# Two-layer hybrid decoder on one core: ACT's weight roundings placed behind evacuations, the pooling mixer pipelined over three advances per pair of up products, the order at attention's start and end changed

## The chip, the core and the metric

One core of one Trainium2 chip runs the whole program. The engines named below are PE (matrix products), DVE (vector), ACT (scalar, activations), POOL (GpSimd) and SP, which issues the DMAs. The metric is the device time of one execution in microseconds (us), taken as the median over executions; a smaller number is better.

## The reference, cut to what matters

Two layers over 1040 tokens (16 meta tokens and 1024 others) of width 1024. Layer 0 mixes with latent attention (16 heads), layer 1 with a pooling mixer of four groups of 256 channels. Behind each mixer stands a gated MLP with a causal convolution of width 3 over the tokens. Every part has an RMS norm before and after it.

```python
for i in range(2):
    a = rmsnorm(h, norm_mix_pre[i])
    m = mla_mixer(a, ...) if i == 0 else pool_mixer(a, w_group, scale)
    h = h + rmsnorm(m, norm_mix_post[i])
    f = conv_ffn(rmsnorm(h, norm_ffn_pre[i]), ...)
    h = h + rmsnorm(f, norm_ffn_post[i])

# pool_mixer, per group g with window w = 2, 4, 8, 16:
means = (csum - csum shifted by w) / min(t, w)
y[g] = (means[g] - h[g]) @ w_group[g]              # 256 x 256
# conv_ffn
u = h @ w_up                                        # 1024 x 5632
u = conv_b + sum(conv_w[j] * up[:, j:j + L] for j in range(3))
gate, val = split(u); return (silu(gate) * val) @ w_down
```

## The kernel before

**Number format.** Every matrix product is made of three: both operands are split into a rounded high part and the rest. For a weight tile, ACT makes the high part (`wh<-wr`, L64), DVE the low part (`wl<-wr,wh`, L70), and PE then runs wh·xh, wh·xl and wl·xh into PSUM (L764).

**Stages, in order.** Down projections of attention (`ps_d`, 5 to 85 us); attention (85 to 545 us), of which `open_attention` returns the opening steps (projections of the first heads) and `attention` runs 48 blocks, three query blocks of up to 348 tokens for each of 16 heads; the output projection `wo(0)` and `wo(1)` (545 to 643 us) for two halves of the tokens (536 and 504); then for each layer and each half: `ffn_up` part 0, `ffn_down` part 0, `ffn_up` part 1, `ffn_down` part 1. A part of `ffn_up` is 11 pairs of products (gate and value), so 22 *up products*. In layer 0, half 1, an up product is 24 matmuls over 506 columns; in layer 1, half 0 it is 48 matmuls over 260 or 262 columns. An up product's PSUM result is taken out by ACT (`cv`, L908: the first tap and the bias) and twice by DVE (`cv<-ps_m`, L912: the other taps); these three are called the evacuation here.

**Attention.** A block's scores (`ps_s`, L534 to L536; `score_tile`), softmax (DVE L543 and L551, ACT L548, POOL L553), transposes (`ps_t`, L585) and value products (`ps_o`, L570 and L571; `value_steps`) are queued so that the scores of the next block stand between the value steps of the present one (`merge`). The scores of block (0, 0) are emitted at the start of `attention`, after the opening steps. The last head's blocks run as 0, 1, 2, so that the last block has nine value steps and no scores beside them. A finished head goes to memory (`heads<-o`, L577) and comes back as operand of `wo` (`or<-heads`, L703). `wo(0)` starts its first three output tiles without the last 128 rows of the operand (`early`).

**Background work.** Norms, residual additions and the pooling mixer are generators (`after_mixer`, `after_ffn`, `post`, `pre`, `poolmix`). `tick()` advances the first of them to its next `yield`, with the priority of an instruction 200 places earlier in the program. Ticks stand between products: two per pair of up products, one per output tile of `ffn_down`, two per tile of `wo`; `drain()` runs the rest between the stages. `poolmix` shapes a group's two 128-channel slices on DVE (`pa` L1027, running sums `psm` L1037, `pmx` L1040, small corrections L1043 and L1044), splits them (`xh` on ACT, `xl` on DVE), and then emits the group's matmuls. It runs twice, each time inside part 0 of the `ffn_up` of that time: for half 0 during layer 0, half 1 (24 matmuls over 268 columns per group; the stretch from 1039 to 1199 us, called pool 1 here), and for half 1 during layer 1, half 0 (12 matmuls over 504 columns per group; 1441 to 1591 us, pool 2).

**What sets the order.** A scheduler walks the program once, with those priorities, and fixes for each engine one queue. At run time an engine takes its queue in order and waits where an operand is late. `issue_after(x)` queues what it holds behind instruction x. In the kernel before, a weight tile's rounding is queued as soon as the scheduler finds room, up to five up products ahead.

**PSUM.** Six banks serve the products: `banks(2)` makes three tiles of two banks, for half 0, `banks(1)` six tiles of one, for half 1.

Of the kernel before, what the change touches and what calls it, by code (L numbers as in the profile page):

```python
# [11 lines left out]
F32 = mybir.dt.float32  # L12
# [8 lines left out]
T = NMETA + SEQ  # L21
# [25 lines left out]
class Kern:  # L47
# [270 lines left out]
    def open_attention(self, es):  # L318
# [12 lines left out]
        return [rs[0], ks[0], rs[1], qs[0], ks[1], *vs[:4], qs[1], rs[2], ks[2], qs[2], *vs[4:]]  # L331
# [8 lines left out]
    def attention(self, es):  # L340
        tc, nc, io = self.tc, self.nc, self.io
        if True:
# [173 lines left out]
    def score_tile(self, h, b, i):  # L516

        nc, ap, sm = self.nc, self.ap, self.aq
# [4 lines left out]
        P = self.aq.tile([QT, min(T, 348 * (b + 1))], F32, tag=f"P{b}", name="P", bufs=3)  # L523
# [35 lines left out]
    def value_steps(self, h, b, P):  # L559
# [19 lines left out]
        def step(j):  # L579
# [13 lines left out]
            if j % self.PM == 1 and not (h == NH - 1 and b == 2):  # L593
# [13 lines left out]
    def dense(self):  # L607
# [3 lines left out]
        self.fp, self.up, self.tp = P("fp", 8), P("up", 2), P("tp", 5)  # L611
# [4 lines left out]
        self.dtile = lambda x: self.tp.tile([128, HALF], F32R, tag="x" + x, name="diag", bufs=2)  # L616
        self.H, self.A, self.bg = {}, {}, []
# [40 lines left out]
    def after_mixer(self, hf, F, acc, L, pre):  # L658
        acc = yield from self.post(hf, F, acc, G_MIXPOST + 8 * L)
        if pre:  # L660

            self.late = yield from self.inv_rms_steps(acc, "xh", 2)
            yield from self.pre(hf, L, True)
        else:
            yield from self.ffn_norm(hf, acc)
# [44 lines left out]
    def wtile(self, src, nk, pool=False):  # L710
        nc = self.nc
        n = 128 * nk
# [11 lines left out]
        self.split(r[:, :n], hi[:, :n], lo[:, :n], lo_eng="dve")  # L724
# [43 lines left out]
    def evac(self, dst, ps, scale=None):  # L768
        c0 = 0
        for p in ps:  # L770
            d = dst[:, c0:c0 + p.shape[1]]
            if scale is None:
                self.nc.scalar.copy(d, p)  # L773
            else:
                self.nc.scalar.activation(d, p, AF.Copy, scale=scale)
            c0 += p.shape[1]

    def addsq(self, acc, t):

# [11 lines left out]
    def wo(self, hf):  # L791
# [14 lines left out]
        for m in range(KD):  # L806
# [3 lines left out]
            else:  # L810
                ps = self.mm_half(self.wtile(io["w_o"][m], KD), *O)
# [3 lines left out]
            self.evac(f, ps)  # L815
# [71 lines left out]
    def ffn_up(self, hf, part):  # L887
# [8 lines left out]
        for jj in range(JH):  # L896
            j = part * JH + jj
            cv = []
            for gv in range(2):
                idx = gv * NJ + j  # L900
                u, = self.mm_half(self.wtile(io["w_up"][L, j, :, gv], KD), ah, al, skip=skip)
                if (L, hf) == (0, 0):
                    t = self.up.tile([128, HALF], F32, tag="u", name="u")
# [4 lines left out]
                nc.scalar.activation(c, u[:, pad:pad + n], AF.Identity, bias=self.par(p0 + 3), scale=self.par(p0 + 2))  # L908
# [18 lines left out]
    def ffn_down(self, part, G, F):  # L927
# [3 lines left out]
        src = lambda m, k0, nk: self.wtile(io["w_down"][L, part, m, :, k0:k0 + nk], nk)  # L931
# [181 lines left out]
```

## Time and profile before

| | us |
|---|---|
| median of 3 runs | 2242.7 (2241.12 to 2243.98) |
| the profiled execution's own time | 2243.88 |
| its span in the trace | 2242.1 |
| PE busy | 2153.3 (96% of the span) |
| DVE busy | 1466.7 (65%) |
| ACT busy | 1045.3 (47%) |
| POOL busy | 382.7 (17%) |

The busy time of an engine is the union of its instructions, so a PE that runs at half its clock is as busy as one at full clock. The granted clock (PEclk) stands beside it: 1.00 is 2.4 GHz, 0.50 is 1.2 GHz, a value between them is a stretch that had both. Over the whole span it is 0.982. Where the queue of PE stands still, the bracket at a row names the instruction that came last before it went on.

### The profile page before, as it was taken

To read this page: it belongs to the slowest core of one execution; us is meant where nothing else is said; L and a number is where in the kernel's file an instruction comes from. 1 tells how busy PE (TensorE), PEld (TensorE's weight loads), DVE (VectorE), ACT (ScalarE), POOL (GpSimd) and SP (SyncE) were. 2 spreads that over 40 slices of the span, in tenths; PEclk is the share of its full clock that TensorE was granted. 3 is DMA by queue.
4 is the path that set the end of the run, shared out by engine and by line. 5 is a ranking of instruction groups with operands and counts; after the bars stand their busy time and mean duration, and the time that the engine had idled before them with its cause. 6 is when DMAs were issued, how large, how long until landed. Compare 5 with 4: busy or idle time off the path is not lost.

```text
span 2242.1 us, 36260 instructions
## 1 busy us (share of the span) xinstructions
PE 2153.3 (96%) x13890; PEld 1971.5 (88%) x13890; DVE 1466.7 (65%) x2713; ACT 1045.3 (47%) x1932; POOL 382.7 (17%) x728
## 2 busy tenths in 40 slices
PE   8889999998999999999998999999899999999996
PEld 8888888887989999999876888899899998888886
DVE  7877777776489726665877565587745557634656
ACT  6377777776464423433544344344434433433431
POOL 5567676764000000000000000000000000000001
PEclk9999999998999999999999999999999999999998
DMA  5011111114343232233322423422242244223231
GB/s 163 25 33 31 30 34 31 25 55 135 113 161 127 80 105 95 80 98 117 94 71 89 134 96 89 128 83 86 74 142 85 77 128 174 94 84 114 94 94 47
DMA packets 82901, 202.74 MB, mean 90 GB/s; under 512 B 10548, under 2 KB 31668, under 8 KB 82728
## 3 DMA queue, kind: packets, MB, share of 16 engines
q1 hardware_dynamic: 82584, 200.18, 28.7%
q8 instruction: 109, 1.79, 0.3%
q14 instruction: 64, 0.52, 0.1%
q10 hardware_dynamic: 144, 0.25, 0.0%
HBM read 179.15 MB, written 16.97 MB: 87 GB/s over the span
## 4 chain that ended last, share of the span: by engine, by line
PE 86%; DVE 5%; ACT 4%; DMA 2%; issue 2%; POOL 2%; DVEq 0%; SPq 0%; POOLq 0%; ACTq 0%
PE ps_m L764 72%; PE ps_t L585 2%; PE ps_s L534 2%; PE ps_o L570 1%; PE ps_s L535 1%; PE ps_s L536 1%; ACT P L548 1%; PE ps_o L571 1%; DMA xt<-in_x 1%; DVE ps_s L543 1%; PE ps_qk L415 1%; PE ps_qk L416 1%; PE ps_qk L417 1%; PE ps_st L84 1%; ACT pth L598 0%
## 5 line engine op out<-in xcount | busy, mean ns | idle before, releaser
L70 DVE TENSOR_TENSOR wl<-wr,wh 128x1024 fp32r<-128x1024 f32 (+3 forms) x316 | 348.4, 1103 | 416.0 <-ACT wh L64 406.8
L64 ACT CAST wh<-wr 128x1024 fp32r<-128x1024 f32 (+3 forms) x316 | 301.2, 953 | 590.3 <-PE ps_m L764 513.1
L764 PE MATMUL ps_m<-ah,wh 128*128 128x506 f32 (+2 forms) x2112 | 565.6, 322 | 3.7 <-DVE cv L912 2.0
L764 PE MATMUL ps_m<-al,wh 128*128 128x506 f32 (+2 forms) x2112 | 568.4, 323 | 0.0
L764 PE MATMUL ps_m<-ah,wl 128*128 128x506 f32 (+2 forms) x2112 | 565.1, 322 | 0.0
L764 PEld LDWEIGHTS ps_m<-ah,wh 128*128 128x128 f32 x2112 | 354.7, 190 | 34.6 <-ACT cv L908 2.2
L764 PEld LDWEIGHTS ps_m<-al,wh 128*128 128x128 f32 x2112 | 354.4, 190 | 27.7
L764 PEld LDWEIGHTS ps_m<-ah,wl 128*128 128x128 f32 x2112 | 354.5, 190 | 27.4
L764 PE MATMUL ps_m<-gh,wh 128*128 128x268 f32 (+3 forms) x1088 | 289.6, 319 | 2.2 <-ACT F L773 2.2
L764 PE MATMUL ps_m<-gl,wh 128*128 128x268 f32 (+3 forms) x1088 | 288.6, 318 | 0.0
L764 PE MATMUL ps_m<-gh,wl 128*128 128x268 f32 (+3 forms) x1088 | 288.5, 318 | 0.0
L912 DVE SCALAR_TENSOR_TENSOR cv<-ps_m,params,cv 128x504 f32<-128x504 f32 (+1 forms) x264 | 196.1, 744 | 3.1
L764 PEld LDWEIGHTS ps_m<-gh,wh 128*128 128x128 f32 x1088 | 184.0, 191 | 15.9 <-ACT F L773 2.4
L764 PEld LDWEIGHTS ps_m<-gh,wl 128*128 128x128 f32 x1088 | 182.9, 190 | 13.6
L764 PEld LDWEIGHTS ps_m<-gl,wh 128*128 128x128 f32 x1088 | 183.3, 190 | 13.1
L64 ACT CAST gh<-cv 128x504 fp32r<-128x504 f32 (+2 forms) x88 | 54.7, 622 | 170.3 <-DVE cv L918 170.3
L548 ACT ACTIVATE P<-ps_s,stat 116x116 f32<-116x116 f32 (+9 forms) x160 | 111.2, 698 | 31.9 <-DVE stat L543 25.0
L585 PE MATMUL ps_t<-ident,P 116*116 116x116 f32 x720 | 114.4, 268 | 11.5 <-DVE ptl L599 6.8
L916 ACT ACTIVATE cv<-cv 128x504 f32<-128x504 f32 (+2 forms) x88 | 55.9, 635 | 139.3 <-DVE cv L912 139.3
L553 POOL TENSOR_SCALAR P<-P,stat 116x116 f32<-116x116 f32 (+2 forms) x144 | 108.7, 757 | 57.5 <-DVE stat L551 49.8
L867 POOL TENSOR_SCALAR al<-ahalo 128x2 fp32r<-128x2 f32 x16 | 5.4, 336 | 631.6 <-PE ps_m L764 631.5
L585 PEld LDWEIGHTS ps_t<-ident,P 116*116 116x116 f32 x720 | 83.9, 136 | 25.8 <-DVE ptl L599 6.7
(201 smaller groups left out, 3605.5 us busy)
## 6 DMA issues: line engine op xcount, KB each, us to landing
wr<-in_w_up SPq DMA_DIRECT2D x176, 512.0 KB, 3.5
wr<-in_w_down SPq DMA_DIRECT2D x56, 384.0 KB, 3.1
wr<-in_w_down SPq DMA_DIRECT2D x56, 320.0 KB, 2.9
wr<-in_w_o SPq DMA_DIRECT2D x16, 512.0 KB, 3.6
resid<-H SPq DMA_DIRECT2D x16, 268.0 KB, 4.1
H<-resid SPq DMA_DIRECT2D x16, 268.0 KB, 3.4
xt<-in_x SPq DMA_DIRECT2D x32, 130.0 KB, 2.4
resid<-H SPq DMA_DIRECT2D x16, 252.0 KB, 3.9
```

Source lines behind the costliest of these rows:

```text
L64: nc.scalar.copy(hi, src)
L70: eng.tensor_tensor(lo, src, hi.bitcast(F32), op=ALU.subtract)
L84: nc.tensor.matmul(ps[:w, i:i + 1], acc[:, w * i:w * i + w], self.ones, start=True, stop=True)
L415: nc.tensor.matmul(ps, wh, xh, start=i == 0, stop=False)
L416: nc.tensor.matmul(ps, wh, xl, start=False, stop=False)
L534: nc.tensor.matmul(ps[:n, x, :w], qh[:, qs], kh[:, ks], start=True, stop=False)
L548: nc.scalar.activation(dst, ps, AF.Exp, bias=mx[:n, 1:2], scale=-1.0, accum_out=es[:n, gi:gi + 1])
L553: nc.gpsimd.tensor_scalar(P[:n, :nk], P[:n, :nk], rs[:n], 1.0, op0=ALU.mult, op1=ALU.mult)
L585: nc.tensor.transpose(pt[:kn, x * QT:x * QT + n], Pi[:n, k0:k0 + kn], self.ident[:n, :n])
L764: nc.tensor.matmul(p, w, x[k][:, skip + c0:skip + c0 + m], start=k == 0 and w is wh and x is xh, stop=k == last and w is wl)
L912: nc.vector.scalar_tensor_tensor(c[:, o:], u[:, pad + x - 2 + o:pad + x - 2 + n], self.par(p0 + x), c[:, o:], op0=ALU.mult, op1=ALU.add)
L916: nc.scalar.activation(c, c, AF.Silu)
```

## The change

**Weight roundings.** `wtile` takes `behind=k`: the rounding of the weight tile is queued behind the k-th last evacuation (`marks`), 3 for most up products, 1 to 3 for `ffn_down`, 3 for `wo`.

**Ticks.** A third tick stands inside the second product of each pair, between its first and second four weight tiles: 33 per part in place of 22.

**Pooling mixer.** `shape(g, kk)` is a function; group g's matmuls are emitted one step later, behind the first slice of group g+1. The tags xh and xl have three buffers, and `u` takes one of them in place of a pool of its own.

**Attention's start.** The three score tiles of block (0, 0) stand among the opening steps.

**Attention's end.** The last head's blocks run as 2, 1, 0.

```diff
-        return [rs[0], ks[0], rs[1], qs[0], ks[1], *vs[:4], qs[1], rs[2], ks[2], qs[2], *vs[4:]]
+        self.first, ss = self.new_scores(0, 0)
+        return [rs[0], ks[0], rs[1], qs[0], ks[1], ss[0], *vs[:2], ss[1], *vs[2:4], ss[2], qs[1],
+                rs[2], ks[2], qs[2], *vs[4:]]
...
-            blocks = [(h, b) for h in range(NH) for b in range(3)]
-            P, steps = self.new_scores(0, 0)
-            run(steps)
+            blocks = [(h, b) for h in range(NH - 1) for b in range(3)] + [(NH - 1, b) for b in (2, 1, 0)]
+            P = self.first
...
-        P = self.aq.tile([QT, min(T, 348 * (b + 1))], F32, tag=f"P{b}", name="P", bufs=3)
+        P = (self.aq if b else self.ap).tile([QT, min(T, 348 * (b + 1))], F32, tag=f"P{b}", name="P", bufs=3)
...
-        self.dtile = lambda x: self.tp.tile([128, HALF], F32R, tag="x" + x, name="diag", bufs=2)
+        self.dtile = lambda x: self.tp.tile([128, HALF], F32R, tag="x" + x, name="diag", bufs=3)
...
-    def wtile(self, src, nk, pool=False):
+    def wtile(self, src, nk, pool=False, behind=0):
         nc = self.nc
+        order = self.tc.issue_after(self.marks[-behind]) if behind else nullcontext()
...
-        self.split(r[:, :n], hi[:, :n], lo[:, :n], lo_eng="dve")
+        with order:
+            self.split(r[:, :n], hi[:, :n], lo[:, :n], lo_eng="dve")
...
-                ps = self.mm_half(self.wtile(io["w_o"][m], KD), *O)
+                ps = self.mm_half(self.wtile(io["w_o"][m], KD, behind=3 if hf or m > 4 else 0), *O)
...
-            self.evac(f, ps)
+            self.marks.append(self.evac(f, ps))
...
-                u, = self.mm_half(self.wtile(io["w_up"][L, j, :, gv], KD), ah, al, skip=skip)
+                W = self.wtile(io["w_up"][L, j, :, gv], KD, behind=2 if jj + gv == 0 else 3)
+                ps = self.mm_half(W[:KD // 2], ah, al, 0, KD, skip=skip, n=n + pad)
+                if gv == 1:
+                    self.tick()
+                u, = self.mm_half(W[KD // 2:], ah, al, KD // 2, KD, ps, skip, n + pad)
                 if (L, hf) == (0, 0):
-                    t = self.up.tile([128, HALF], F32, tag="u", name="u")
+                    t = self.tp.tile([128, HALF], F32, tag="xl", name="u", bufs=3)
...
-                nc.scalar.activation(c, u[:, pad:pad + n], AF.Identity, bias=self.par(p0 + 3), scale=self.par(p0 + 2))
+                i = nc.scalar.activation(c, u[:, pad:pad + n], AF.Identity, bias=self.par(p0 + 3),
+                                         scale=self.par(p0 + 2))
+                self.marks.append(getattr(i, "ins", i))
...
-        for g in range(4):
+        def shape(g, kk):
...
-                xh.append(hi_)
-                xl.append(lo_)
-                if kk == 0:
-                    W = self.wtile(io["w_pool"][g], 4, True)
-                yield
-            for m in range(2):
-                ps = self.mm_half([W[2 * kk + m] for kk in range(2)], xh, xl)
...
-                acc = self.addsq(acc, f)
-            yield
+        X = [([], []) for _ in range(4)]
+        W = None
+        for g in range(5):
+            for kk in range(2):
+                if g < 4:
+                    for dst, t in zip(X[g], shape(g, kk)):
+                        dst.append(t)
+                    yield
+                if g and kk == 0:
+                    for m in range(2):
+                        ps = self.mm_half([W[2 * x + m] for x in range(2)], *X[g - 1])
+                        f = self.fp.tile([128, HALF], F32, tag="F", name="F")[:, :n_tok]
+                        self.evac(f, ps, self.par(G_PS + 2 * (g - 1) + m))
+                        F.append(f)
+                        acc = self.addsq(acc, f)
+                if g < 4 and kk == 0:
+                    W = self.wtile(io["w_pool"][g], 4, True)
+        yield
         return F, acc
```

What the queues make of it is seen at three places. The lines of the changed kernel are numbered a little higher (L764 is L770 there, L912 is L927, L1027 is L1044).

**ACT at the end of `wo(1)`**, where `F<-ps_m` takes an output tile out of PSUM and `wh<-wr` rounds a weight tile. Before, the last two tiles:

```order
L64 CAST wh<-wr 128x1024
L773 COPY F<-ps_m 128x504
L786 ACTIVATE sq<-H 128x536 x2
L64 CAST wh<-wr 128x1024
L773 COPY F<-ps_m 128x504
L786 ACTIVATE sq<-F 128x504 x4
L64 CAST wh<-wr 128x1024 x2
```

Of the change, the last three tiles:

```order
L779 COPY F<-ps_m 128x504
L794 ACTIVATE sq<-F 128x504
L779 COPY F<-ps_m 128x504
L64 CAST wh<-wr 128x1024 x2
L794 ACTIVATE sq<-F 128x504
L779 COPY F<-ps_m 128x504
L64 CAST wh<-wr 128x1024
L130 COPY R<-ps_bc 128x268
```

Before, a rounding stands right ahead of each of the last two copies; now the seventh copy comes first with two roundings behind it, and the third rounding stands behind the eighth copy.

**PE in pool 1**, around the broadcast `ps_bc` of the pre-mixer norm (the operand of all shapes, made from DVE's `diag`). Before, it stands inside the 13th up product, and the first group's matmuls (`xh,pwh`) follow only behind the 15th; here it stands between rows of up products:

```order
L764 MATMUL ps_m<-ah,wl 128x506
L126 MATMUL ps_bc<-diag,ones_r 128x268 x4
L764 MATMUL ps_m<-ah,wh 128x506
L764 MATMUL ps_m<-al,wh 128x506
L764 MATMUL ps_m<-ah,wl 128x506
```

Of the change, right behind the 11th up product:

```order
L770 MATMUL ps_m<-ah,wl 128x506
L126 MATMUL ps_bc<-diag,ones_r 128x268 x4
L770 MATMUL ps_m<-xh,pwh 128x268 x4
L770 MATMUL ps_m<-ah,wh 128x506
L770 MATMUL ps_m<-al,wh 128x506
```

The broadcast and the first matmuls of group 0 now follow each other, ahead of the 12th product. Further on, ahead of the 15th product, the rest of group 1, all of group 2 and the first four matmuls of group 3 stand together.

**DVE in pool 1**, at the first shapes. Before, `cv` evacuations and weight roundings stand between them:

```order
L1027 SCALAR_TENSOR_TENSOR pa<-H,params,R 128x536
L1037 TENSOR_TENSOR psm<-pa 128x551
L70 TENSOR_TENSOR wl<-wr,wh 128x1024
L912 SCALAR_TENSOR_TENSOR cv<-ps_m,params,cv 128x504
L1040 SCALAR_TENSOR_TENSOR pmx<-psm,pa 128x536
L1027 SCALAR_TENSOR_TENSOR pa<-H,params,R 128x536
L912 SCALAR_TENSOR_TENSOR cv<-ps_m,params,cv 128x504
L1043 TENSOR_TENSOR pmx<-psm,params 128x16
```

Of the change, between the evacuations of the 11th and the 12th product:

```order
L117 TENSOR_TENSOR diag<-ident,yl 67x536
L1044 SCALAR_TENSOR_TENSOR pa<-H,params,R 128x536
L1054 TENSOR_TENSOR psm<-pa 128x551
L1057 SCALAR_TENSOR_TENSOR pmx<-psm,pa 128x536
L1044 SCALAR_TENSOR_TENSOR pa<-H,params,R 128x536
L1060 TENSOR_TENSOR pmx<-psm,params 128x16
L1054 TENSOR_TENSOR psm<-pa 128x551
L1061 TENSOR_TENSOR pmx<-pmx,pa 128x16
L1057 SCALAR_TENSOR_TENSOR pmx<-psm,pa 128x536
L1044 SCALAR_TENSOR_TENSOR pa<-H,params,R 128x536
L70 TENSOR_TENSOR xl<-pmx,xh 128x536
```

Three of the eight slices are shaped there in one piece; the eighth is done before the 15th product is evacuated.

## Rows read from the trace of the kernel before

**Rows 1.** The page: busy times by engine, and the chain by line.

```profile
PE 2153.3 (96%) x13890; PEld 1971.5 (88%) x13890; DVE 1466.7 (65%) x2713; ACT 1045.3 (47%) x1932; POOL 382.7 (17%) x728
...
PE ps_m L764 72%; PE ps_t L585 2%; PE ps_s L534 2%; PE ps_o L570 1%; PE ps_s L535 1%; PE ps_s L536 1%; ACT P L548 1%; PE ps_o L571 1%; DMA xt<-in_x 1%; DVE ps_s L543 1%; PE ps_qk L415 1%; PE ps_qk L416 1%; PE ps_qk L417 1%; PE ps_st L84 1%; ACT pth L598 0%
```

**Rows 2.** Waits of PE: what it waited for, total us, times, longest.

```profile
PE ps_m L764 <- ACT xh L64: 17.2, 4, 10.1
PE ps_bc L126 <- DVE diag L117: 8.2, 5, 3.9
...
PE ps_m L764 <- ACT F L773: 3.6, 2, 2.2
```

**Rows 3.** Stretches: length, busy us (count) of PE, PEld, DVE, ACT, POOL, PEclk, DMA, GB/s.

```profile
85.00:135.00 50.00, 38.52 (x213) 34.87 (x213) 41.80 (x112) 25.41 (x70) 31.86 (x45) 0.83 0.12 32
200.00:250.00 50.00, 47.33 (x320) 42.68 (x319) 35.63 (x102) 34.97 (x96) 34.46 (x65) 1.00 0.15 37
500.00:545.00 45.00, 37.86 (x229) 32.52 (x227) 33.47 (x82) 33.08 (x84) 26.86 (x61) 0.90 0.34 104
800.00:900.00 100.00, 100.00 (x811) 100.00 (x811) 47.66 (x56) 34.36 (x43) 0.00 (x0) 1.00 0.31 98
1056.00:1100.00 44.00, 44.00 (x198) 36.36 (x197) 40.34 (x56) 23.23 (x35) 0.11 (x1) 1.00 0.31 97
1100.00:1200.00 100.00, 85.46 (x403) 71.68 (x403) 77.39 (x133) 43.15 (x72) 2.75 (x15) 0.91 0.21 63
1190.20:1194.80 4.60, 4.60 (x13) 3.88 (x14) 3.76 (x7) 0.64 (x1) 0.00 (x0) 0.50 0.00 0
1441.00:1460.00 19.00, 19.00 (x157) 18.92 (x156) 13.39 (x29) 6.33 (x9) 0.00 (x0) 1.00 0.33 108
1540.00:1600.00 60.00, 56.35 (x405) 53.52 (x404) 48.79 (x73) 27.10 (x43) 3.41 (x4) 0.94 0.22 66
```

**Rows 4.** Timeline of PE, rows behind long waits: start, us, row, idle before and releaser.

```profile
122.84 0.38 PE L534 MATMUL ps_s<-kh,qh 96*116 96x256 f32 x1 [1.19 <-ACT P L548]
...
131.84 0.43 PE L570 MATMUL ps_o<-pth,v 116*128 116x348 f32 x1 [0.44 <-ACT pth L598]
...
529.66 0.66 PE L570 MATMUL ps_o<-pth,v 116*128 116x348 f32 x1 [1.97 <-DVE o L576]
...
1190.13 1.26 PE L764 MATMUL ps_m<-xh,pwh 128*128 128x268 f32 x4 [10.13 <-ACT xh L64]
...
1473.48 0.48 PE L764 MATMUL ps_m<-ah,wh 128*128 128x260 f32 x2 [1.99 <-DVE cv L912]
```

**Rows 5.** Timeline of ACT at the end of the output projection's second half.

```profile
641.37 1.04 ACT L64 CAST wh<-wr 128x1024 fp32r<-128x1024 f32 x1 [2.59 <-PE ps_m L764]
642.32 0.57 ACT L773 COPY F<-ps_m 128x504 f32<-128x504 f32 x1
```

**Rows 6.** DVE's groups by form, 1039 to 1205 us: count, busy us, mean ns, idle before.

```profile
L912 DVE SCALAR_TENSOR_TENSOR cv<-ps_m,params,cv 128x504 f32<-128x504 f32 x44 | 32.4, 738 | 0.2
L70 DVE TENSOR_TENSOR wl<-wr,wh 128x1024 fp32r<-128x1024 f32 x19 | 23.2, 1221 | 9.9 <-ACT wh L64 9.9
L1027 DVE SCALAR_TENSOR_TENSOR pa<-H,params,R 128x536 f32<-128x536 f32 x8 | 6.2, 771 | 0.3 <-ACT R L130 0.3
L70 DVE TENSOR_TENSOR xl<-pmx,xh 128x536 fp32r<-128x536 f32 x8 | 5.7, 714 | 1.7 <-ACT xh L64 1.6
L1040 DVE SCALAR_TENSOR_TENSOR pmx<-psm,pa 128x536 f32<-128x536 f32 x8 | 5.7, 712 | 0.1
L1037 DVE TENSOR_TENSOR psm<-psm 128x549 f32<-128x549 f32 x6 | 4.3, 723 | 0.0
L1043 DVE TENSOR_TENSOR pmx<-psm,params 128x16 f32<-128x16 f32 x8 | 1.4, 169 | 0.0
```

**Rows 7.** DMA issues of the page: count, KB each, us to landing.

```profile
heads<-o SPq DMA_DIRECT2D x32, 87.0 KB, 2.1
...
or<-heads SPq DMA_DIRECT2D x8, 268.0 KB, 2.7
```

More of the change, by code (lines that the diff above doesn't have):

```diff
@@ L1 @@
-from contextlib import ExitStack
+from contextlib import ExitStack, nullcontext
 import numpy as np
@@ L516, in score_tile @@
     def score_tile(self, h, b, i):
[L518 removed]
+        nc, sm = self.nc, self.ap
         qh, ql = self.qt[h]
@@ L592, in step @@
                 nc.gpsimd.memset(tl[:kn, r0:e0].bitcast(F32), 0.0)
-            if j % self.PM == 1 and not (h == NH - 1 and b == 2):
+            if j % self.PM == 1 and not (h == NH - 1 and b == 0):
                 tf = self.aq.tile([QT, 348], F32, tag="ptf", name="ptf", bufs=1)
@@ L660, in after_mixer @@
         if pre:
-            self.late = yield from self.inv_rms_steps(acc, "xh", 2)
+            self.late = yield from self.inv_rms_steps(acc, "xh", 3)
             yield from self.pre(hf, L, True)
@@ L772, in evac @@
             if scale is None:
-                self.nc.scalar.copy(d, p)
+                i = self.nc.scalar.copy(d, p)
             else:
-                self.nc.scalar.activation(d, p, AF.Copy, scale=scale)
+                i = self.nc.scalar.activation(d, p, AF.Copy, scale=scale)
             c0 += p.shape[1]
+        return getattr(i, "ins", i)
     def addsq(self, acc, t):
@@ new lines, in shape @@
+            k = 2 * g + kk
+            a = self.tp.tile([128, HALF + 16], F32, tag="tc", name="pa")[:, :end]
+            if hf == 0:
+                nc.gpsimd.memset(a[:, :16], 0.0)
+            else:
+                nc.gpsimd.tensor_scalar(a[:, :16], self.phalo[:, k], 1.0, 0.0, op0=ALU.mult, op1=ALU.add)
+            nc.vector.scalar_tensor_tensor(a[:, 16:], self.H[hf][k], self.par(G_MIXPRE + 8 + k), R,
+                                           op0=ALU.mult, op1=ALU.mult)
+            if hf == 0:
+                nc.gpsimd.tensor_scalar(self.phalo[:, k], a[:, n_tok:end], 1.0, 0.0,
+                                        op0=ALU.mult, op1=ALU.add)
@@ new lines, in shape @@
+            s = a
+            for l in range(g + 1):
+                d = 1 << l
+                lo, hi = 2 * d - 1, end
+                n = self.tp.tile([128, HALF + 16], F32, tag="tc", name="psm")[:, :end]
+                nc.vector.tensor_tensor(n[:, lo:hi], s[:, lo:hi], s[:, lo - d:hi - d], op=ALU.add)
+                s = n
+            mx = self.tp.tile([128, HALF + 16], F32, tag="tc", name="pmx")[:, :end]
+            nc.vector.scalar_tensor_tensor(mx[:, 16:], s[:, 16:], 1.0 / win, a[:, 16:],
+                                           op0=ALU.mult, op1=ALU.subtract)
@@ new lines, in shape @@
+            if hf == 0:
+                nc.vector.tensor_tensor(mx[:, 16:32], s[:, 16:32], self.par(G_CNT + 16 * g, 16), op=ALU.mult)
+                nc.vector.tensor_tensor(mx[:, 16:32], mx[:, 16:32], a[:, 16:32], op=ALU.subtract)
+            hi_ = self.tp.tile([128, HALF], F32R, tag="xh", name="xh", bufs=3)[:, :n_tok]
+            lo_ = self.tp.tile([128, HALF], F32R, tag="xl", name="xl", bufs=3)[:, :n_tok]
+            self.split(mx[:, 16:], hi_, lo_, lo_eng="dve")
+            return hi_, lo_
```

53 lines of the change are left out of this document (13 added, 40 removed).

## The prediction, on record before the changed kernel was run

> **What bounds the kernel now.** I read the page first. PE is busy for 96% of the span, and the chain that ended last lies on PE's product line for 72% of it [rows 1]; DVE is at 65%. A kernel in this state can gain only where PE stands still or runs at half its clock, so I looked next at the waits of PE. Three of them concern the change: 17.2 us for the pooling mixer's `xh`, 8.2 us for `diag` and 3.6 us for copies out of PSUM [rows 2]. The third view cuts the program into stretches [rows 3]. Where PE runs freely, 811 matmuls take 100 us (0.123 us each over 268 columns), 198 take 44 us (with a few tiny ones among them; I use 0.229 for 506 columns), 157 take 19 us (0.121 for 260). Between 1100 and 1200 us PE is idle for 14.5 us, and its mean clock is 0.91.
>
> I price a bad stretch by two parts: the idle time, and half of the time in which PE works at half clock. The reader should see that they overlap: the 4.6 us behind the longest wait have a clock of 0.50 with PE fully busy [rows 3], and that wait itself was 10.1 us [rows 4]. Pool 1 lost 14.5 us idle; of the 18 us of half clock (twice 0.09 x 100) some 6 lay in the wait, so 12 x 0.5 = 6 is the clock's part: 20.5 in all. It has three of the four waits for `xh` [rows 2], so a fall of the clock costs 2 us on the mean; for one behind a short wait I take 1.7. Pool 2 lost 3.7 + about 3 = 7 between 1540 and 1600.
>
> The Trainium skill's page "TensorE: Matmul & The Clock Gate", section Terms, puts the penalty of throttling at the whole throttled time times (1 − K/N). By that rule pool 1's clock part would be 18 x 0.5 = 9 and not 6; the rows say less, as half clock costs nothing while PE waits.
>
> **The change part by part.**
>
> *Attention's start.* From 85 to 135 us PE is idle for 11.5 us at a clock of 0.83, while a steady stretch of 50 us has 2.7 idle and 1.00 [rows 3]. So about 9 idle plus some 6 of clock are above normal. Part of this is the first scores: the waits from 122.84 to 131.84 [rows 4] are the first and the last of five, 3.4 us together, as each score tile had nothing beside it. With the scores among the opening steps these 3.4 us go, with one fall of the clock (1.7), and nine matmuls can fill 1 us of the 3.9 us wait for `diag` [rows 2]. Against it, DVE gets three more softmax steps inside the chain that ends in that `diag`. Bounds: nothing to −9. I take −5, near the rows at 121 to 132.
>
> *Attention's end.* From 500 to 545 us idle is 7.1 at 0.90; normal would be 2.4 idle. The excess is 4.7 idle + 0.10 x 45 x 0.84 = 3.8 of clock, and the wait of 1.97 at 529.66 [rows 4] lies in it: 8.5. The cause is nine value steps of the last block with no scores between. With blocks 2, 1, 0 three value steps stay uncovered, a third. What comes late instead is the last head, which `wo(0)` needs: store 2.1 and load 2.7 [rows 7], and four rows of ACT and DVE (copy, sum, two for the split) of 0.5 to 0.7, as the like rows of [rows 6]; together 7 us. Its cover is three tiles of 42 matmuls, 126 x 0.123 = 15.5 us, so it is hidden; without that cover it would cost the 7 us. Bounds −2 to −8.5; I take two thirds, −6.
>
> *Weight roundings.* In the steady stretches PE has no idle time, so nothing can be won there. Three evacuations stood behind a rounding or other work. At 641 us ACT rounds (1.04 us) ahead of the last copy [rows 5]; PE waits for it, 1.4 of the 3.6 us in two waits [rows 2]. The new order has the copy ahead: −1.4 (0 to −1.4). The other of the two, 2.2 us, is at 1621 us: PE waits for a copy, as ACT stands behind DVE's residual work there; in the change that work has moved ahead into `ffn_up`. It gives 2.2 and a fall of the clock (1.7): −3.9 (0 to −3.9). At 1473 PE waits 1.99 for `cv` on DVE [rows 4]; the residual additions ahead of it stay, spread a little more: −1.8 (0 to −3.7). The price is a shorter lead: weights were up to five products ahead, now two to three. Two products are 2 x 24 x 0.229 = 11 us, and one rounding costs 1.05 on ACT and 1.2 on DVE [rows 6]. Only a block of DVE work of over 10 us in front of a `wl` would show. The longest ones are in pool 1, priced next; outside I take 0 (to +3).
>
> *Pool 1.* This is the dear term. In the changed queues all eight slices are shaped between the evacuations of products 11 and 15. I counted DVE's instructions there: 8 `pa`, 20 `psm`, 8 `pmx`, 8 `xl`, 16 small ones, 3 pool weight parts and 2 `diag` (0.7 each, as the rows of their width), and the usual 8 `cv`, 4 `wl`, 2 + 2 for the gate product and 5 `acc` (0.7). With the means of [rows 6]: 6.2 + 14.5 + 5.7 + 5.7 + 2.7 + 2.1 + 1.4 + 5.9 + 4.9 + 2.7 + 3.5 + 0.5 (tiny ones of the norm) = 55.8 us. Back to back they follow each other up to 0.07 us sooner than their durations; for the 58 or so independent ones that gives 52. PE has in the same time 4 x 5.5 + 76 x 0.123 + 0.5 = 32 us. PE can't run ahead: `ps_bc` right behind product 11 waits for `diag`, which DVE makes after that product's evacuation, and in front of products 12 and 15 stand pool matmuls whose `xh` is made inside those blocks. So PE must stand for 20 to 24 us plus 1.3 for the hop DVE–PE–ACT–DVE at `ps_bc`: about 10 at product 11 and 13 at product 14. Two falls of the clock add 2 x 1.7 to 2.5. Sum 25 to 30 in place of 20.5. Before, the same work was spread over products 12 to 22 and the drain, with one block (group 2) that gave the 10.1 us. I take +6.5 (−1 to +10; the lower end if every DVE row runs at its shortest spacing).
>
> The Trainium skill, "PSUM — Partial Sum Buffer", section Engine vs sequencer instructions, says that DVE's queue is strict FIFO and that matmuls run in program order. That speaks against this change, and if PE or DVE could pass over what is late, pool 1 would cost nothing and the sum would be 27 us lower.
>
> *Pool 2.* In the same way: between the evacuations of products 8 and 15, DVE has 14 `cv`, 7 `wl` and 56 others that are 504 to 520 columns wide (I take 0.69): 10.3 + 8.5 + 38.6 = 57 us by the means, 54 with the shorter spacing. PE has 7 x 48 x 0.121 + 48 x 0.229 = 52. The difference of 2 to 5, the hop 1.3 and two to three falls of 1.7 give 7 to 11 against 7, and PE can't spread the difference evenly, as its pool matmuls stand in bunches here too: +3 (−3 to +8).
>
> *The rest.* The third tick itself issues nothing; three buffers of xh and xl take away waits that the trace doesn't show. The residual work that moves from `ffn_down` into `ffn_up` makes a DVE block at product 19 of pool 1 (8 scalings, 8 additions, two `wl`, two `cv`: about 15 us), but six PSUM tiles let PE run 5 products (27 us) on: 0.
>
> **Sum.** −5 − 6 − 1.4 − 3.9 − 1.8 + 6.5 + 3 = −8.6 us. The profiled execution took 2243.9 and would come to 2235.3; it lies 1.2 over the median 2242.7 of the runs, off which the forecast is **2234 us**.
>
> **The rivals.**
>
> 1. *The mixer is hidden after all.* With 33 advances the DVE work fits beside PE, as the three-buffer tags let it run ahead, and pool 1 and 2 lose 5 us each in place of 20.5 and 7. For it: DVE is busy for 77 of 100 us there [rows 3], so there is room on average. Against it: the queues put it all in four products. Time: the pools give −17.5 in place of +9.5, and the rest −18, so about 2207.
>
> 2. *Slower: DVE becomes the bound in the pool stretch, and PE starves for more than the blocks' difference.* The place is the 23 us block between the evacuations of products 14 and 15: a `pwl` waits for the matmuls of the group before (one buffer), these for `xl`, and so DVE also stands still, 2 to 3 us per group. Over four groups in both pools that is some 20 us, so the pools cost +29 in place of +9.5. It decides where they cost more than the 18 us that the rest gives: 2243 + 29 − 18 = 2254.
>
> 3. *Gain and loss cancel.* The opening scores only move the wait to `diag`, since the DVE chain grows by three softmax steps (2 us or more), and the end of attention waits for the last head; start and end then give −3 together. Time: −3 − 7 + 9.5 = 0, 2243.
>
> **How the numbers follow.** This kernel can be told from no change by about 0.2%, 4.5 us. Chances: the forecast (to 2238) 0.58, rival 1 and cases between it and the forecast 0.06, rival 3 (2238 to 2247) 0.22, rival 2 0.14. So faster 0.64, same 0.22, slower 0.14. The range 2221 to 2248 leaves out rival 1 and most of rival 2, under 2 in 10; the forecast's own range is 2225 to 2242, its bounds taken at half their width.
>
> **What would show it right or wrong.** In the changed profile: a wait of PE at `ps_bc` or `xh` of about 10 us in pool 1 behind product 11 and one of 10 to 14 us, in one or two pieces, behind product 14, each with half clock after it; no wait for a copy at 641 and 1621; none of over 0.5 us for `ps_s` among the first scores; at attention's end one fall of the clock at most, and no wait for `oh` or `ol` in `wo(0)`. Wrong would be: pool 1 with under 15 us idle (the count of DVE work is off, or the queue has slack that I missed), or over 30; or an idle PE in the steady `ffn_up` parts in front of `wl` rows (the shorter lead costs).

## The result, and the profile of the changed kernel

The changed kernel takes 2265.4 us (2264.0 to 2266.7, 5 runs) against 2242.5 of the kernel before: ratio 1.0097, interval 1.0086 to 1.0109. It is 23 us slower; the forecast was 2234, the range 2221 to 2248. The profiled execution has a span of 2263.9 us (2242.1 before).

The page first, its busy times (answers to [rows 1]):

```profile
PE 2155.7 (95%) x13890; PEld 1969.4 (87%) x13890; DVE 1455.9 (64%) x2711; ACT 1033.6 (46%) x1932; POOL 390.5 (17%) x732
```

PE does the same work; the 22 us more are lost around it. The waits of PE by what ended them (answers to [rows 2]; total, times, longest):

```profile
PE ps_m L770 <- ACT xh L64: 19.8, 7, 5.3
PE ps_m L770 <- ACT wh L64: 14.7, 4, 9.1
PE ps_bc L126 <- DVE diag L117: 10.8, 5, 4.6
...
PE ps_m L770 <- DVE xl L70: 5.2, 4, 1.7
...
PE ps_m L770 <- ACT F L779: 2.2, 2, 2.0
```

The second row is new. The list of before has no such row of 0.7 us or more; now PE waits for a weight's rounding for 14.7 us, once for 9.1. The waits for `xh` are seven in place of four, none longer than 5.3. The stretches (columns as in [rows 3]), with one at the end of the output projection:

```profile
85.00:135.00 50.00, 39.95 (x229) 36.02 (x228) 42.74 (x118) 27.59 (x74) 33.03 (x46) 0.86 0.13 33
500.00:545.00 45.00, 37.11 (x223) 31.79 (x223) 30.66 (x75) 31.19 (x77) 25.61 (x57) 0.89 0.31 93
1100.00:1200.00 100.00, 78.44 (x365) 65.32 (x364) 77.75 (x142) 40.69 (x67) 8.18 (x15) 0.83 0.18 60
600.00:625.00 25.00, 14.03 (x68) 10.85 (x68) 16.65 (x35) 7.69 (x13) 0.00 (x0) 0.77 0.23 88
```

Attention's start has 10.1 us idle in place of 11.5, its end 7.9 in place of 7.1; pool 1 has 21.6 in place of 14.5, at a clock of 0.83 in place of 0.91. From 600 to 625 us PE worked for only 14 us. To put every kernel below on one scale I summed, per stage, by how much the starts of PE's matmuls stand further apart than matmuls of the same form usually do in the trace before (the 30th percentile). This holds waits and half clock together; the sum over all stages differs by some 22 us between the two kernels, as their spans do. A loss is that of the one execution that was profiled, which lies up to 5.5 us from the median of its kernel; in two runs that leave `wo` as the change has it (fewer sums, two ticks) that stage lost some 23.5 where the changed kernel lost 20.2, so a difference of 3 us in one stage says little. *First up* is part 0 of layer 0, half 0.

```
us lost          attention  wo    first  up with  down    up with  down
                                  up     pool 1   behind  pool 2   behind
before             95.9     5.7    2.4    20.2     2.4     12.2     6.8
changed            91.2    20.2    2.5    33.9     0.5     18.2     1.2
difference         -4.7   +14.5   +0.1   +13.7    -1.9     +6.0    -5.6
```

Two stages carry the loss: `wo` (the output projection, 545 to 643 us before) and the up part with pool 1. In `wo`, these are PE's row behind its longest wait and ACT's rows at the same time (start, us, row, idle before):

```profile
620.18 0.79 PE L770 MATMUL ps_m<-oh,wh 128*128 128x504 f32 x1 [9.07 <-ACT wh L64]
```

```profile
611.03 0.67 ACT L130 COPY R<-ps_bc 128x268 f32<-128x268 f32 x2 [15.83 <-PE ps_bc L126]
617.98 0.58 ACT L779 COPY F<-ps_m 128x504 f32<-128x504 f32 x1 [6.28 <-DVE H L847]
618.45 0.74 ACT L883 ACTIVATE ah<-H,params 128x536 fp32r<-128x536 f32 x1
619.10 1.03 ACT L64 CAST wh<-wr 128x1024 fp32r<-128x1024 f32 x1
```

and DVE's:

```profile
611.73 5.59 DVE L842 SCALAR_TENSOR_TENSOR F<-F,params,R 128x536 f32<-128x536 f32 x8 [5.86 <-ACT R L130]
617.23 5.10 DVE L847 TENSOR_TENSOR H<-H,F 128x536 f32<-128x536 f32 x8
```

Read from below: PE waits for `wh`, the rounding of the second half's fourth weight tile (619.10). It stands on ACT behind the copy `F<-ps_m` at 617.98, its mark. That copy's product had long been in PSUM (the run with other buffers, below, has the copy at 603); it waited 6.3 us for DVE's `H<-H,F`. There are eight F buffers, the first half's residual work holds all of them, and the copy goes into the first that comes free. Before, that copy was as late, but four roundings went ahead of it, and PE used its six PSUM tiles to run on:

```profile
601.24 1.05 ACT L64 CAST wh<-wr 128x1024 fp32r<-128x1024 f32 x1 [3.22 <-PE ps_m L764]
607.74 1.05 ACT L64 CAST wh<-wr 128x1024 fp32r<-128x1024 f32 x1 [5.46 <-PE ps_m L764]
613.41 0.67 ACT L130 COPY R<-ps_bc 128x268 f32<-128x268 f32 x2 [4.62 <-PE ps_bc L126]
613.97 1.06 ACT L64 CAST wh<-wr 128x1024 fp32r<-128x1024 f32 x1
619.28 1.05 ACT L64 CAST wh<-wr 128x1024 fp32r<-128x1024 f32 x1 [4.26 <-PE ps_m L764]
620.36 0.58 ACT L773 COPY F<-ps_m 128x504 f32<-128x504 f32 x1
```

In pool 1 of the changed kernel, PE's rows behind waits:

```profile
1116.34 1.44 PE L126 MATMUL ps_bc<-diag,ones_r 67*128 67x268 f32 x4 [4.63 <-DVE diag L117]
1123.06 1.26 PE L770 MATMUL ps_m<-xh,pwh 128*128 128x268 f32 x4 [5.27 <-ACT xh L64]
...
1154.42 1.26 PE L770 MATMUL ps_m<-xh,pwh 128*128 128x268 f32 x4 [4.65 <-ACT xh L64]
...
1161.83 1.26 PE L770 MATMUL ps_m<-xh,pwh 128*128 128x268 f32 x4 [2.31 <-ACT xh L64]
...
1167.05 1.26 PE L770 MATMUL ps_m<-xh,pwh 128*128 128x268 f32 x4 [2.16 <-ACT xh L64]
```

The first two stand behind the 11th up product (9.9 us together), the others, with two shorter waits left out here, between the 14th and the 15th.

### The profile page after: what moved, and what is told of

Read it like the earlier page. It is cut to its first block, busy times and chain, and to the rows that moved or that the text cites. A ratio compares the mean times of both kernels' runs of the same rounds, so it can differ in the third digit from the quotient of the medians.

```text
span 2263.9 us, 36293 instructions
## 1 busy us (share of the span) xinstructions
PE 2155.7 (95%) x13890; PEld 1969.4 (87%) x13890; DVE 1455.9 (64%) x2711; ACT 1033.6 (46%) x1932; POOL 390.5 (17%) x732
## 5 line engine op out<-in xcount | busy, mean ns | idle before, releaser
L770 PE MATMUL ps_m<-al,wh 128*128 128x506 f32 (+2 forms) x2112 | 568.6, 323 | 0.0
L770 PE MATMUL ps_m<-ah,wh 128*128 128x506 f32 (+2 forms) x2112 | 566.1, 322 | 2.0 <-ACT wh L64 1.8
L770 PE MATMUL ps_m<-ah,wl 128*128 128x506 f32 (+2 forms) x2112 | 564.5, 322 | 0.0
L70 DVE TENSOR_TENSOR wl<-wr,wh 128x1024 fp32r<-128x1024 f32 (+3 forms) x316 | 343.7, 1099 | 195.7 <-ACT wh L64 195.1
L770 PEld LDWEIGHTS ps_m<-ah,wh 128*128 128x128 f32 x2112 | 355.3, 190 | 33.5 <-ACT wh L64 2.1
L770 PEld LDWEIGHTS ps_m<-ah,wl 128*128 128x128 f32 x2112 | 354.9, 190 | 27.8
L770 PEld LDWEIGHTS ps_m<-al,wh 128*128 128x128 f32 x2112 | 354.7, 190 | 28.0
L927 DVE SCALAR_TENSOR_TENSOR cv<-ps_m,params,cv 128x504 f32<-128x504 f32 (+1 forms) x264 | 196.6, 748 | 191.7 <-ACT cv L921 188.6
L64 ACT CAST wh<-wr 128x1024 fp32r<-128x1024 f32 (+3 forms) x316 | 293.6, 945 | 55.0 <-PE ps_m L770 34.4
L770 PE MATMUL ps_m<-gh,wh 128*128 128x268 f32 (+3 forms) x1088 | 286.6, 316 | 0.0
L770 PE MATMUL ps_m<-gl,wh 128*128 128x268 f32 (+3 forms) x1088 | 285.9, 316 | 0.0
L770 PE MATMUL ps_m<-gh,wl 128*128 128x268 f32 (+3 forms) x1088 | 285.9, 316 | 0.0
L921 ACT ACTIVATE cv<-ps_m,params 128x504 f32<-128x504 f32 (+1 forms) x132 | 102.5, 777 | 234.8 <-PE ps_m L770 234.5
L770 PEld LDWEIGHTS ps_m<-gh,wh 128*128 128x128 f32 x1088 | 181.7, 189 | 13.1
L770 PEld LDWEIGHTS ps_m<-gh,wl 128*128 128x128 f32 x1088 | 181.1, 188 | 13.5
L770 PEld LDWEIGHTS ps_m<-gl,wh 128*128 128x128 f32 x1088 | 181.4, 188 | 13.1
L550 ACT ACTIVATE P<-ps_s,stat 116x812 f32<-116x812 f32 (+9 forms) x160 | 111.4, 698 | 34.2 <-DVE stat L545 26.3
L779 ACT COPY F<-ps_m 128x504 f32<-128x504 f32 (+3 forms) x56 | 28.6, 532 | 198.6 <-PE ps_m L770 192.3
```

Of the source, the lines that this page charges most:

```text
L64: nc.scalar.copy(hi, src)
L70: eng.tensor_tensor(lo, src, hi.bitcast(F32), op=ALU.subtract)
L550: nc.scalar.activation(dst, ps, AF.Exp, bias=mx[:n, 1:2], scale=-1.0, accum_out=es[:n, gi:gi + 1])
L770: nc.tensor.matmul(p, w, x[k][:, skip + c0:skip + c0 + m], start=k == 0 and w is wh and x is xh, stop=k == last and w is wl)
L779: i = self.nc.scalar.copy(d, p)
L921: i = nc.scalar.activation(c, u[:, pad:pad + n], AF.Identity, bias=self.par(p0 + 3), scale=self.par(p0 + 2))
```

## The experiments

Times are medians in us; the ratio is to the kernel before, run on the same chip. Losses are measured as in the table above.

The expectations number the theories. 1: in `wo` a rounding placed behind a copy waits as long as the copy does. 2: PE's waits in the pools are DVE's work, bunched. 3: what attention's new end gains, the start of `wo` gives back. 4: as theory 1, in the down projections behind the pools. 5: the third tick makes the bunches, not the pipelining.

### The output projection

**Roundings free in `wo` alone.** `behind=3 if hf or m > 4 else 0` becomes `behind=0`.

> The changed kernel with the output projection's weight roundings placed freely again (behind=0 in wo alone). Theory 1: in the second half of the output projection the rounding of the fourth weight tile stands behind the copy of the first output tile, and that copy waits until a residual addition of the first half gives its F buffer free, 9 us too late; then the stretch from 550 to 650 us loses 2 to 3 us in place of 17 and the time is 2250 us (2247 to 2253). Rival: the stall is the norm and residual work of the first half, which moved to another place in that stage and blocks ACT and DVE whatever the roundings do; then it stays at 2263 to 2267.

Measured: 2261.6, ratio 1.0075 (1.0052 to 1.0097). In `wo` the loss fell from 20.2 to 9.6, as theory 1 says, but the first up stage rose from 2.5 to 10.4. So theory 1 holds for the place and fails on the total (2250 was expected). The four executions took 2256.0 to 2265.1, and the profiled one is among the two long ones. A loss in the first up stage, which the changed kernel doesn't have, comes out when the stall goes (below).

**Marks in `wo` alone, in the kernel before.** The same line and `marks`, with all else as before.

> The kernel before with nothing but the marks and behind=3 in the output projection. Theory 1: 15 us of stall come, less the 1.4 us wait at 641 us: 2256 us (2252 to 2260). Rival (the moved norm needs other parts of the change): 2240 to 2245.

Measured: 2258.1, ratio 1.0068 (1.0053 to 1.0083); 20.4 lost in `wo` and nothing else moved by over 1.5. One line of the change makes the whole stall.

**Other buffers for the copies.** In the changed kernel:

```diff
-            f = self.fp.tile([128, HALF], F32, tag="F", name="F")[:, :HALVES[hf][1]]
+            pool, tag = (self.gp, f"gh{8 + m}") if hf and m < 3 else (self.fp, "F")
+            f = pool.tile([128, HALF], F32, tag=tag, name="F")[:, :HALVES[hf][1]]
```

> The changed kernel, in which the first three output tiles of the output projection's second half go into buffers that are free there (those of the gate products 8 to 10), so that their copies wait for no residual addition; the roundings stay behind the copies. Theory 1: the 9.1 us wait for the rounding goes, and that stage loses 8 us in place of 20; part of it comes back in the next stage, where the run with free roundings lost 10 in place of 2.5: 2257 us (2252 to 2262). Rival (the roundings are late for ACT's own work or the moved norm): the stage still loses 17 or more, 2263 to 2268.

Measured: 2264.3, ratio 1.0098 (1.0082 to 1.0113). ACT's rows:

```profile
602.87 0.58 ACT L779 COPY F<-ps_m 128x504 f32<-128x504 f32 x1 [3.46 <-PE ps_m L770]
603.34 1.05 ACT L64 CAST wh<-wr 128x1024 fp32r<-128x1024 f32 x1
609.38 0.58 ACT L779 COPY F<-ps_m 128x504 f32<-128x504 f32 x1 [4.46 <-PE ps_m L770]
609.86 1.05 ACT L64 CAST wh<-wr 128x1024 fp32r<-128x1024 f32 x1
```

The copy now comes 15 us sooner, when its product is done, with the rounding right behind it. The 9.1 us wait is gone and `wo` loses 10.7. So the buffer was the cause of that wait. The total stayed, above the range that I gave, as the first up stage lost 12.5.

**Behind the product, not its copy.**

```diff
-            self.marks.append(self.evac(f, ps))
+            self.evac(f, ps)
+            self.marks.append(self.lastmm)     # last matmul of the product
```

> The changed kernel, in which the output projection's roundings are placed behind the last matmul of the product three back and not behind its copy. Theory 1: the rounding no longer waits for a late copy, the stage loses 8 to 10 us in place of 20 and the next stage gets part of it back: 2257 us (2252 to 2262). Rival: being placed at all is what delays them; 2263 or more.

Measured: 2260.7, ratio 1.0085 (1.0071 to 1.0099); `wo` 6.7, first up stage 12.0. In `wo`, to be placed behind a product costs nothing (free roundings lost 9.6); to be placed behind what may wait for a buffer does.

### Roundings of the up and down projections

**Roundings placed there alone, in the kernel before.**

> The kernel before with nothing but the marks and placed roundings of the up and down projections. Theory 4 (a rounding behind an evacuation that itself waits for a buffer): in the down projections behind the pools the copies wait for F buffers that the residual work holds, and the roundings wait with them, +13 and +5.5 as in the run without the pipelined mixer: 2261 us (2257 to 2265). Rival: that stall came from the other parts there; 2240 to 2246.

Measured: 2264.7, ratio 1.0099 (1.0082 to 1.0116). The down stage behind pool 1 loses 14.3 in place of 2.4, the one behind pool 2 11.8 in place of 6.8, and the pools stay as they were. The cost is where theory 4 puts it; its cause, the buffer, was tried in `wo` alone.

**The changed kernel with mixer, ticks and buffers of before.**

> The changed kernel with the pooling mixer, the ticks and the buffers of before. Theories 1 and 2: attention -5, output projection +14, pools as before: 2251 us (2247 to 2256). If the placed roundings alone make the pools slower (rival to theory 2), 2262 or more.

Measured: 2275.6, ratio 1.0144 (1.0129 to 1.0159), slower than the changed kernel, and 25 over my expectation: 15.8 and 12.3 in the two down stages, which I hadn't expected since the changed kernel loses nothing there. The time lies in the range of the rival, but the pools lose about 20 and 12 as before, so it isn't the rival's reason. The changed kernel's pipelined mixer or its ticks had covered a price of its own roundings.

**The changed kernel with two ticks per pair**, to tell which of the two it was. The two lines of the third tick are taken out.

> The changed kernel with two ticks per pair. If the pipelining has removed the stall of the down projections behind the pools, the time is the changed kernel's less 20 us in the pools and first up stage: 2245 us (2240 to 2250). If it was the tick, 13 and 5 us of stall come back there: 2261 us (2256 to 2267).

Measured: 2258.3, ratio 1.0065 (1.0050 to 1.0080). The pools fall to 12.4 and 12.1, and the down stages rise to 12.3 and 6.2: it was the tick. With 33 advances the residual work behind the mixer ends inside the up part. PE's row in the down stage and ACT's show a picture like that in `wo`:

```profile
1226.61 0.79 PE L770 MATMUL ps_m<-gh,wh 128*128 128x504 f32 x1 [7.04 <-ACT wh L64]
```

```profile
1217.87 0.67 ACT L130 COPY R<-ps_bc 128x268 f32<-128x268 f32 x2 [14.25 <-PE ps_bc L126]
1224.82 0.65 ACT L790 ACTIVATE acc<-H 128x536 f32<-128x536 f32 x1 [6.28 <-DVE H L847]
1225.37 0.56 ACT L779 COPY F<-ps_m 128x504 f32<-128x504 f32 x1
1225.83 0.73 ACT L64 CAST wh<-wr 128x640 fp32r<-128x640 f32 x1
```

PE waits for the rounding at 1225.83, the rounding stands behind the copy at 1225.37, and the copy behind `acc<-H`, which waits for DVE's `H`. The first `H` also sets the first F buffer free, so these rows don't tell the copy's place in the queue from a wait for its buffer.

### The pooling mixer

**Ticks, pipelining and buffers alone, in the kernel before.**

> The kernel before with nothing but the third tick, the pipelined pooling mixer and the three buffers. Theory 2: the bunching of the shapes comes from the ticks and the new order of emission alone; pool 1 costs 11.5 us more than before, pool 2 4.6 more, the wait at 1621 us is gone (-4): 2254 us (2250 to 2258). Rival: the bunches need the roundings' shorter lead beside them, as DVE must fill the time with something; without it the pools cost what they did: 2238 to 2244.

Measured: 2261.2, ratio 1.0082 (1.0067 to 1.0097), 3 over the upper end. The pool parts lose 29.7 and 19.5, which is theory 2. But the first up stage loses 9.1 in place of 2.4, as in three of the runs on `wo`. PE's rows there:

```profile
710.82 1.04 PE L84 MATMUL ps_st<-ones,acc 128*126 128x1 f32 x8
...
716.00 1.38 PE L126 MATMUL ps_bc<-diag,ones_r 126*128 126x504 f32 x2 [4.15 <-DVE diag L117]
```

The sum `ps_st` of a norm and its broadcast `ps_bc` follow each other with no product between (3 to 17 matmuls in the three others), so PE waits for DVE's chain from the one to the other. Before, 144 matmuls stand between them, in the changed kernel 51, over 7 us.

**Less work in the mixer.** In the changed kernel, only the first running sum of each slice, so that every window is 2: `for l in range(g + 1)` becomes `range(1)`.

> The changed kernel without the running sums behind the first, in every group (the pooling windows are all 2, 12 sums per half are left out). Theory 2: PE's waits in the pools are DVE's work, so 12 x 0.72 = 8.6 us less work give 8 us in pool 1 and 5 to 8 in pool 2: 2251 us (2248 to 2255). Rival: the waits come from the one buffer of the pool weights and the PSUM ring, which the sums don't touch: 2260 or more.

Measured: 2254.3, ratio 1.0060 (1.0044 to 1.0076). The pool parts lose 26.5 and 11.7 in place of 33.9 and 18.2: 7.4 and 6.5 for 8.6 us of DVE work, which neither the weights' buffer nor the PSUM ring would give. Most of what DVE is spared there, PE is spared.

**Pipelining with two ticks, in the kernel before.**

> The kernel before with the pipelined pooling mixer and three buffers, but two ticks per pair as before; its queues put the first group's matmuls behind the 15th up product as before, and spread the shapes over products 13 to 22. Theory 5: it is the third tick that bunches the shapes into four products, not the pipelining; without it pool 1 loses 13 us in place of 20 (before) and 34 (changed kernel): 2236 us (2231 to 2240). Rival: the pipelining itself bunches them; 2250 or more.

Measured: 2228.8, ratio 0.9941 (0.9929 to 0.9954): faster, by more than I expected. The stretch of pool 1, and PE's rows behind waits:

```profile
1100.00:1200.00 100.00, 93.90 (x450) 78.86 (x449) 81.74 (x150) 46.01 (x76) 7.41 (x15) 0.95 0.24 70
```

```profile
1166.68 0.76 PE L769 MATMUL ps_m<-xh,pwh 128*128 128x268 f32 x4 [2.30 <-ACT xh L64]
1169.07 0.82 PE L769 MATMUL ps_m<-xl,pwh 128*128 128x268 f32 x2 [1.63 <-DVE xl L70]
...
1173.39 1.26 PE L769 MATMUL ps_m<-xh,pwh 128*128 128x268 f32 x4 [2.16 <-ACT xh L64]
```

Three waits of 1.6 to 2.3 us stand where the kernel before had one of 10.1 [rows 4]. The pool part loses 11.7 in place of 20.2, and the down stages lose 2 and 5 less; the residual additions end some 5 and 9 us sooner after the start of those stages.

**The third tick alone, in the kernel before.**

> The kernel before with nothing but the third tick. Theory 5: each advance comes after two thirds of a product and not after a whole one, so PE meets every step of the norms and of the mixer before DVE is through: pool 1 loses 40 us or so, the first up stage 8 to 10 in place of 2.4: 2268 us (2256 to 2280). Rival (the tick costs only together with the pipelining): 2240 to 2246.

Measured: 2270.2, ratio 1.0122 (1.0105 to 1.0138). The pool parts lose 41.7 and 23.3. Its stretch of pool 1:

```profile
1100.00:1200.00 100.00, 71.02 (x332) 59.70 (x333) 67.73 (x123) 36.87 (x62) 2.76 (x15) 0.85 0.17 56
```

The first up stage stays at 2.4, which I got wrong.

**Running sums on GpSimd**, in the kernel before with the ends of attention: `(nc.gpsimd if l else nc.vector).tensor_tensor(...)`.

> The same, and in the pooling mixer the running sums behind the first go to GpSimd, 12 of 20 per half. Theory 2 (the pools are bound by DVE's work): 8.6 us of DVE leave each pool, the wait of 10 us in pool 1 shrinks to 3 to 6: 2234 us (2229 to 2238). Rival: GpSimd's sums are longer (0.91 us for 344 columns in attention, so an estimated 1.4 for 549) and stand in the chain to xh; then the waits stay and the time is 2241 or more.

Measured: 2251.2, ratio 1.0044 (1.0027 to 1.0060), 9 us over the ends alone (2242.0, below). The rival holds; the longest wait of pool 1 is 12.4 us in place of 10.1:

```profile
L1052 POOL TENSOR_TENSOR psm<-psm 128x549 f32<-128x549 f32 x6 | 7.9, 1309 | 7.5 <-DVE psm L1052 6.1 <-DVE pmx L1059 1.4
L1052 POOL TENSOR_TENSOR psm<-psm 128x545 f32<-128x545 f32 x4 | 6.0, 1500 | 0.3
```

A sum takes 1.3 to 1.5 us there and 0.72 on DVE [rows 6], and it stands in the chain to `xh`. The Trainium skill's "GPSIMD Engine Reference", section 3.1, gives a ratio of 1.96 for such an add; here it is 1.8 to 2.1, so trace and page agree.

### Attention's start and end

**Both, in the kernel before.**

> The kernel before with nothing but the reordered start and end of attention. By the changed kernel's trace attention itself gives 4.8 us, but the first matmuls of the output projection wait for the last head. Theory 3: 4 us come back there, as in the run with free roundings in the output projection (9.6 us lost in that stage against 5.7): 2241 us (2239 to 2243). Rival, my prediction's reading: nothing comes back and all 8 to 11 us stand: 2233 us.

Measured: 2242.0, ratio 1.0001 (0.9992 to 1.0010). Attention loses 3.1 less, `wo` 2.2 more, both about what one execution can differ from another. PE's waits from 530 to 570 us:

```profile
PE ps_m L770 <- ACT wh L64: 2.4, 1, 2.4
PE ps_o L572 <- DVE o L578: 2.1, 2, 1.4
PE ps_m L770 <- ACT F L779: 2.0, 1, 2.0
PE ps_m L770 <- DVE o L578: 1.1, 1, 1.1
```

PE waits there for a weight's rounding, for the last head's copy `o` and for a copy of the first tiles; in the changed kernel those tiles' copies stand on ACT behind the rounding of a head that comes from memory:

```profile
561.16 0.61 ACT L64 CAST oh<-or 128x504 fp32r<-128x504 f32 x1 [3.44 <-DMA or<-heads]
561.68 1.04 ACT L64 CAST wh<-wr 128x1024 fp32r<-128x1024 f32 x1
562.74 1.81 ACT L779 COPY F<-ps_m 128x268 f32<-128x268 f32 x6
```

**Both, with the pipelined mixer at two ticks.**

> The same as the run with the pipelined mixer at two ticks, and attention's reordered start and end beside it, which alone gave nothing that could be measured: 2236 us (2230 to 2240), equal to the run without them within 2 us.

Measured: 2226.5, ratio 0.9932 (0.9920 to 0.9944), the fastest of all with its neighbour below; without the ends it was 2228.8. The intervals of the ratios overlap, but on the same chip all five executions with the ends (2225.6 to 2227.0) lie under all five without (2227.7 to 2229.1), so some 2 us of gain are likely there, where the ends alone showed none.

**The same with placed roundings in the up projections.**

> The fastest version so far (pipelined mixer at two ticks, attention's start and end) with placed roundings in the up projections alone. No copy into an F buffer stands there ahead of a rounding, except at a stage's first two tiles, so theory 4 expects nothing: 2226 us (2223 to 2230). Rival: the shorter lead costs by itself, 2232 or more.

Measured: 2228.7 (2223.5 to 2229.6), ratio 0.9928 (0.9913 to 0.9943): no difference in the whole. In pool 2 a wait of 1.8 us for a rounding, behind the fourth up product, replaces one of 2.0 for `cv` behind the fifth. So the shorter lead costs nothing that can be measured where no mark waits for a buffer.

## Why the prediction was wrong

**Weight roundings** is the step that failed. I priced the shorter lead by DVE blocks in front of a `wl`, gave 0 (to +3) outside the pools, and took −1.4 in the output projection. I looked for a late `wl` of DVE, where ACT's `wh` came late, and treated an evacuation as something that comes at its product's end. In `wo(1)` it doesn't: the copies wait for F buffers, and a rounding behind them waits too. It measured +14.5 in that stage, the 1.4 included (+14.7 with the marks in `wo` alone). ACT's queue shows it: I looked at the end of `wo(1)` there and not at its start. Runs with the marks alone, with other buffers and with marks on the product agree on it. A price of the same kind stands in the down stages (+12 and +5 alone), where the third tick covered it: so the changed kernel shows −1.9 and −5.6 there, of which I had forecast −3.9 at 1621 us.

**Pool 1** was right in mechanism and too small in size: +6.5 (−1 to +10) was predicted, +13.7 came, +11.8 with the down stage behind it. The count of DVE's work holds: 50 us busy were measured from 1111 to 1172 us, for 52 to 56. So do the waits behind product 11 (9.9 us for "about 10") and 14 (9.1 in the rows shown, 11.7 with two shorter ones, for 13). What was short is the clock's part: I took 2 x 1.7 to 2.5, 3.4 to 5 us, as for two falls. There were two, but both lasted: the rows show 0.83 over 100 us, that is 34 us at half clock, while several waits of 2 to 5 us follow each other. 33.9 lost less 21.6 idle leave some 12. The stretches, columns as in [rows 3]:

```profile
1115.30:1128.70 13.40, 7.09 (x19) 5.71 (x20) 11.01 (x24) 2.58 (x5) 1.28 (x6) 0.50 0.07 20
1152.80:1173.10 20.30, 12.52 (x40) 10.56 (x41) 19.28 (x33) 6.13 (x13) 5.90 (x5) 0.50 0.21 76
```

By the rule of the Trainium skill that the prediction weighed ("TensorE: Matmul & The Clock Gate", section Terms) the clock's part would be an estimated half of 34, 17; rows and rule differ in the same direction as before.

**The third tick** I said issues nothing and costs nothing by itself. It issues nothing, but it brings the steps so close that PE waits for each: alone it costs 26 us, while the pipelining with its third buffers, at two ticks, gives 13. I had read the bunched order correctly and put it down to the mixer as a whole.

**Pool 2 and the stage behind it**: +3 − 1.8 − 3.9 = −2.7 predicted, +6.0 − 5.6 = +0.4 measured. The wait for `cv` at 1473 is gone, but one product sooner PE now waits as long for a rounding, so its −1.8 fell:

```profile
1488.90 0.48 PE L770 MATMUL ps_m<-ah,wh 128*128 128x260 f32 x2 [1.80 <-ACT wh L64]
```

It is the only wait of that kind in pool 2, and every run with placed up roundings has it: there the shorter lead shows, at about the price of the wait that it replaced.

**Attention**: −11 predicted, −4.7 measured in the stage, and the ends alone give nothing. At the start the five waits of the first scores (3.4 us) went as said and the wait of 3.9 for `diag` fell to 2.1, but new ones of 0.9 (for the first scores, where I said none over 0.5) and 1.6 us stand among the opening steps, so that the idle time fell by 1.4 us in all. At the end the cover for the last head exists, but ACT's queue puts copies of the first tiles behind the head's rounding, so that PE waits for those, 2 us, and for the first tile's rounding, 1.9 us. My own rival 3 had this ("the end of attention waits for the last head").

The sum of the steps was −8.6; by the stages it came to +22. Some 16 us of the difference are the roundings in `wo`, 5 pool 1, 3 pool 2 and 6 attention. The direction was right for pool 1 and wrong for the whole: the stall that I hadn't priced, +14.5, is larger than all gains together, −12.2. Yet with `wo` as I had it the sum of the stages would still be +6, some 2249 us, just outside my range; pool 1, pool 2 and attention each came out worse than I had taken them.

**What stays open.** Why the first up stage loses 7 to 10 us more in four runs (mixer with tick alone, free roundings, other buffers, marks on the product). All four have the third tick and the pipelined mixer with its buffers, and no stall in `wo`; the norm's sum and its broadcast stand 0 to 17 matmuls apart in them. With the tick alone there are 144 between them, with the mixer and buffers at two ticks 81, with both and the stall (the changed kernel) 51, and nothing is lost. So it takes both. The mixer itself doesn't run in that stage, which leaves its third buffers, one of which `u` takes there; no run tests that.

## What to carry to other kernels

Before work is queued behind an instruction, ask what that instruction may wait for itself: a copy out of PSUM needs a free destination as well as a finished product. Mark the product if the order is all that is wanted.

The distance between two steps of background work is a size to be set, as a buffer count is. A step more per pair of products made the same work slower, since the main queue met each step before the engine beside it was through; emitting the consumer one step later made it faster. Parts of a change can pay for each other, so one part alone, and all but one, are both worth a run: here the fastest kernels hold the pipelined mixer without its third tick, and none of the roundings placed in `wo`.

## What the runs showed of the hardware beyond the expected

The clock's price depends on how the waits lie. In the kernel before one wait of 10.1 us and two short ones cost 6 us of clock; in the changed one seven waits of 0.8 to 5.3 us had 34 us at half clock and cost some 12, although the idle time was only 1.5 times as long (21.6 against 14.5). From 1146 to 1172 us the granted clock was 0.63 with PE busy for 14.4 of 26 us:

```profile
1146.00:1172.00 26.00, 14.35 (x54) 11.65 (x54) 25.27 (x43) 11.60 (x23) 6.01 (x6) 0.63 0.23 81
```
